# Short-convolution sums in PSUM, long taps in channel pairs, VectorE alone subtracting late in the mixers, router constants split

## The chip, the cores and the metric

The kernel runs on one core of a Trainium2 chip. The metric is the device time of one execution in microseconds, lower is better. Each kernel is timed several times; the median is quoted.

## What is computed

One layer of a streaming encoder on 256 tokens of 1024 channels. Three token mixers read the same input, are merged by sigmoid gates, and pass through one output projection; after a layer norm a routed mixture of 16 experts follows. The part that the change touches:

```python
a = a_val * jax.nn.sigmoid(a_gate)                       # mixer A
a = causal_depthwise_conv(a, conv_a_w) + conv_a_b        # 31 taps
a = jax.nn.silu(layer_norm(a, ln_a_g, ln_a_b))
y_a = jnp.einsum("btc,cd->btd", a, w_a_out)

yb = gate_bb * causal_depthwise_conv(gate_cc * xb, conv_b_w)   # mixer B, 3 taps
y_b = jnp.einsum("btc,cd->btd", yb, w_b_out)

merged = g[..., 0, :] * y_a + g[..., 1, :] * y_b + g[..., 2, :] * y_c
return jnp.einsum("btd,de->bte", merged, w_o) + b_o
```

Mixer C (trailing means, then a grouped projection) gives `y_c`. The router's logits, after the first layer norm, are computed with the norm's gain and shift folded into constants, which `router_consts` makes from the weights alone.

## The kernel before

Channels lie on partitions, in 8 tiles of 128; a row of a tile is the 256 tokens. The mixers run over 49 weight chunks of 1 MB each (list `MIX`), one block of TensorE work per chunk: blocks 0 to 7 are A (each gives value and gate of one channel tile), 8 to 11 are C, then X0 X1 B0 X2 X3 B1 X4 X5 B2 X6 X7 B3 (blocks 12 to 23: an X block gives `gate_cc` and `xb` of one tile, a B block `gate_bb` of two), WC (24), four rounds of two gate blocks and one WB (25 to 36), four more gate blocks G0 (37 to 40), WA0 and WA1 (41, 42), WO0, WA2, WA3, WO1 to WO3 (43 to 48). The experts follow.

Precision is kept by splitting float32 into two halves of a narrower kind: for each chunk, `convert(j + 2, CUT)` at block j has ScalarE copy the high half (line 162), and GpSimd and VectorE subtract it from the raw chunk (line 172) into a low half. Of the 2048 columns of a chunk GpSimd takes the first `CUT` = 1280 (1024 + 256), VectorE the other 768. A block (`proj`) is then 48 matmuls of 128x256: high by high, high by low (line 314) and low by high (line 319), into one PSUM bank of the tag `pj`, of which there are four. A later block can only start when the bank that it reuses has been read.

Who reads the bank of a block:

- A: ScalarE's sigmoid, then VectorE's product (line 346) into `UP`. Of each second A block, 62 conv taps (31 for each of two channel tiles) are queued in `later["V"]`: line 333 for the first tap, 336 for the others. After every block `drain("V", ...)` emits some of the queued taps; how many is a budget of 5.0 us less VectorE's subtraction and less `COST[kind]`. The sum of a channel tile stands in a PSUM bank of its own, tag `z`, `CA[i]`, four banks in turn.
- X (`ev_X`): ScalarE adds a bias (line 393), VectorE multiplies (line 396, this frees the bank), then makes the 3-tap convolution in SBUF: line 400 for the first tap, 402 for the two others.
- B (`ev_B`): VectorE, two instructions at line 407, from the bank times the convolution; then ScalarE and GpSimd split the product.

Mixer A's layer norm (`ln_a`) is placed by `LNA` = 32: the mean's matmul after block 33, centring (lines 458, 459) at block 34, the sum of squares (463) at 35, the variance matmul (468) behind block 35, the scaling (473 to 481) at block 36 and the eight swish steps (`swish`: lines 486 and 487 on VectorE, split by ScalarE at 266 and GpSimd at 267 into `AH` and `AL`) behind blocks 36 and 37. WA0, block 41, is the first to read `AH` and `AL`. `load_res`, `residual` (line 555) and `router_consts` (products and sums on VectorE, 563 to 567, one matmul, 569, and two small operations behind it) hang on `LNA` as well: `router_consts` runs behind block 40.

In the mixers a scheduler orders the instructions of each engine by its own estimate of when they can run; in the experts the order is the program's. Weights are loaded by SyncE's queue, a chunk as soon as the slot of an earlier one is free.

Of the kernel before, what the change touches and what calls it, by code (L numbers as in the profile page):

```python
# [12 lines left out]
AF = mybir.ActivationFunctionType  # L13
OP = mybir.AluOpType
# [3 lines left out]
T = 256  # L18
D = 1024
KT = 8  # L20
NE = 16
# [8 lines left out]
PB, PCW, PCB, PLG, PLB, PBW, PCS, PRT, P1G, P1B = 0, 72, 320, 328, 336, 344, 368, 376, 504, 512  # L30
# [82 lines left out]
def body(ctx, tc, w, xt, x, par, rows, out):  # L113
    nc = tc.nc
    V, S, G, PE = nc.vector, nc.scalar, nc.gpsimd, nc.tensor
# [6 lines left out]
    def slot(tag, shape, dt=F32):  # L122
        nm[0] += 1
        return big.tile(shape, dt, name=f"{tag}_{nm[0]}", tag=tag)

    def t2k(shape, dt=F32, tag="t2k", bufs=5):
        nm[0] += 1
        return tmp.tile(shape, dt, name=f"{tag}_{nm[0]}", tag=tag, bufs=bufs)

    def bank(tag="pj", shape=(128, 2, 256)):  # L130
        nm[0] += 1
        return ps.tile(list(shape), F32, name=f"{tag}_{nm[0]}", tag=tag, bufs=4)
# [19 lines left out]
    def hi(j, a, b, step=512, eng=None):  # L152

        if j not in htag:
            htag[j] = (hfree or free).pop(0)
            HI[j] = slot(htag[j], [128, 2048], F32R)
        for i in range(a, b, step):
            o = slice(i, min(i + step, b))
            if eng:
                eng.tensor_copy(HI[j][:, o], raw[j][:, o])  # L160
            else:
                S.activation(HI[j][:, o], raw[j][:, o], AF.Copy)  # L162

    def lo(j, eng, a, b, step=512):

        if j not in LO:
            ltag[j] = (lfree or free).pop(0)
            LO[j] = slot(ltag[j], [128, 2048], F32R)
        for i in range(a, b, step):
            o = slice(i, min(i + step, b))  # L170
            left[j] = left.get(j, 2048) - (o.stop - o.start)
            eng.tensor_tensor(LO[j][:, o], raw[j][:, o], HI[j][:, o].bitcast(F32), op=OP.subtract)  # L172
        if j in left and left[j] == 0:
            del raw[j], left[j]
            give(tags[j])

    def convert(j, cut, step=1024, half=None):

        if j not in raw:
            return  # L180
        for e in (0, 1) if half is None else (half,):
            a, m, b = 1024 * e, 1024 * e + min(1024, max(0, cut - 1024 * e)), 1024 * e + 1024
            hi(j, a, b, step)
            lo(j, G, a, m, step)
            lo(j, V, m, b, step)
# [33 lines left out]
    def col(base, i):  # L219
        return P[:, base + i:base + i + 1]  # L220
# [44 lines left out]
    def halves(dh, dl, src, eng):  # L265
        S.activation(dh, src, AF.Copy)  # L266
        eng.tensor_tensor(dl, src, dh.bitcast(F32), op=OP.subtract)  # L267
# [17 lines left out]
    def put(eng, cost, f):  # L285
        later[eng].append((cost, f))
# [35 lines left out]

    ssum = [None]

    CA = {}

    def conv_tap(i, k):

        src = UP[:, i, k:k + T]
        wk = P[:, PCW + i * TAPS + k:PCW + i * TAPS + k + 1]  # L330
        if k == 0:
            CA[i] = bank("z", (128, T))
            V.tensor_scalar(CA[i], src, wk, col(PCB, i), op0=OP.mult, op1=OP.add)
        else:
            ca = CA[i]
            V.scalar_tensor_tensor(AC[:, i] if k == TAPS - 1 else ca, src, wk, ca, op0=OP.mult, op1=OP.add)  # L336
        if k == TAPS - 1 and i == 1:
            ssum[0] = t2k([128, T], tag="ssum", bufs=2)
            put("G", 0.6, lambda: G.tensor_tensor(ssum[0], AC[:, 0], AC[:, 1], op=OP.add))
        elif k == TAPS - 1 and i:  # L340
            put("G", 0.6, lambda: G.tensor_tensor(ssum[0], ssum[0], AC[:, i], op=OP.add))
# [41 lines left out]
            put("G", 1.25, lambda lev=lev: add(lev))  # L383
        put("G", 10, mean)

    yconv = {}
    Y = {}

    def ev_X(i, p):
        if i == 0:  # L390
            Y["h"], Y["l"] = slot("YH", [128, KT, T], F32R), slot("YL", [128, KT, T], F32R)
        cc = t2k([128, T])
        S.activation(cc, p[:, 0], AF.Identity, bias=col(PB, 24 + i))
        u = t2k([128, 2 + T])
        G.memset(u[:, :2], 0.0)
        V.scalar_tensor_tensor(u[:, 2:], p[:, 1], col(PB, 32 + i), cc, op0=OP.add, op1=OP.mult)  # L396
        if i % 2 == 0:
            yconv[i // 2] = t2k([128, 2, T])
        y = yconv[i // 2][:, i % 2]
        V.tensor_scalar(y, u[:, :T], col(PBW, 3 * i), None, op0=OP.mult)  # L400
        for k in (1, 2):
            V.scalar_tensor_tensor(y, u[:, k:k + T], col(PBW, 3 * i + k), y, op0=OP.mult, op1=OP.add)

    def ev_B(q, p):
        y = yconv.pop(q)
        for n in range(2):
            V.scalar_tensor_tensor(y[:, n], p[:, n], col(PB, 16 + 2 * q + n), y[:, n], op0=OP.add, op1=OP.mult)
        halves(Y["h"][:, 2 * q:2 * q + 2], Y["l"][:, 2 * q:2 * q + 2], y, G)

    MS = {}  # L410
# [86 lines left out]
    A = {}  # L497
# [26 lines left out]

    done = None
    CUT = 1280
    LNA = 32
    extra, blk = {}, [0]

    def at(j, f, after=False):  # L530

        extra.setdefault((j, after), []).append(f)

    COST = {"A": .45, "C": .7, "X": 1.3, "B": .9, "WB": .7, "WA": 1.3}

    R1 = {}

# [19 lines left out]
    RT = {}  # L557

    def router_consts():

        gw = RT["w"] = const.tile([128, KT, NE], F32, name="gw")
        wr = P[:, PRT:PRT + 128].rearrange("p (k e) -> p k e", e=NE)
        V.tensor_tensor(gw, wr, P[:, P1G:P1G + KT, None].to_broadcast([128, KT, NE]), op=OP.mult)
        bw, bs = t2k([128, KT, NE]), t2k([128, 2, NE])
        V.tensor_tensor(bw, wr, P[:, P1B:P1B + KT, None].to_broadcast([128, KT, NE]), op=OP.mult)
        V.tensor_reduce(bs[:, 0], bw.rearrange("p k e -> p e k"), axis=AX.X, op=OP.add)
        V.tensor_reduce(bs[:, 1], gw.rearrange("p k e -> p e k"), axis=AX.X, op=OP.add)
        pb = bank("pj", (128, 2, NE))
        PE.matmul(pb, ones, bs, start=True, stop=True)
        RT["b"] = const.tile([128, NE], F32, name="rb")  # L570
        V.scalar_tensor_tensor(RT["b"], pb[:, 0], float(D), R1["br"], op0=OP.mult, op1=OP.add)
        RT["s"] = const.tile([128, NE], F32, name="rs")
        V.tensor_scalar(RT["s"], pb[:, 1], float(D), None, op0=OP.mult)

    cost = 0
    for j, c in enumerate(MIX):
        kind, n = c
        blk[0] = j
        if j + 2 < NM:
            convert(j + 2, CUT)  # L580
        if done:
            done()
            done = None
        for f in extra.pop((j, False), ()):
            f()
        cost = 0
        if kind == "WC":
            wc_block(j)
        elif kind == "WO":
            if n == 0:  # L590
                for t in range(2):
                    for half in range(2):
                        wo(j, n, t, half)
        else:
            ah, al = {"WA": lambda: (A["h"], A["l"]), "WB": lambda: (Y["h"], Y["l"])}.get(kind, lambda: (XH, XL))()
            p = proj(j, ah, al)
            f = {"A": ev_A, "C": ev_C, "X": ev_X, "B": ev_B, "WA": ev_WA, "WB": ev_WB}.get(kind)
            done = (lambda f=f, n=n, p=p: f(n, p)) if f else (lambda b=int(kind[1]), n=n, p=p: gate(b, n, p))
            cost = COST.get(kind, 0)
        for f in extra.pop((j, True), ()):  # L600
            f()
        drain("V", 5.0 - (2048 - CUT) * 1.04e-3 - cost)
        drain("G", 5.0 - CUT * 2.2e-3)
        if j == LNA:
            drain("V", 1000)
            drain("G", 1000)
            at(j + 1, lambda: ln_a(LNA + 2), True)
        if j == LNA + 6:
            load_res()
            at(j + 2, router_consts, True)  # L610
            at(j + 2, scaled_identity, True)
            at(j + 3, lambda: residual(0), True)
            at(j + 4, lambda: (residual(1), give("AC")), True)
        if c == ("G0", 3):
            give("XH", "XL")
        if c == ("WA", 3):
            give("AH", "AL")
        if c == ("WO", 1):
            give("PL", "M")
# [437 lines left out]
    j = NM  # L1057
# [47 lines left out]
    for e in range(NE + 1):  # L1105
        if e < NE:
            while e // 2 not in ready:
                some()
            p = bank("pj", (128, 512))
# [64 lines left out]
    y = t2k([128, 512])  # L1174
# [47 lines left out]
    with tc.If(over > CAP):  # L1222
        xs, xt_ = slot(free.pop(0), [128, 2, D]), slot(free.pop(0), [128, KT, T])
        V.tensor_tensor(xs, XX["h"].bitcast(F32), XX["l"].bitcast(F32), op=OP.add)
        z = slot(free.pop(0), [128, 2, D])
# [4 lines left out]
        for t in range(2):  # L1230
            for h in range(2):
                p = bank("pj", (128, 4, 128))
# [3 lines left out]
        for e in range(NE):  # L1236
# [4 lines left out]
            for t in range(2):  # L1241
                gu = []
                for kind in ("EG", "EU"):
                    p = bank("pj", (128, 512))
# [9 lines left out]
                p = bank("pj", (128, 4, 128))  # L1254
# [3 lines left out]
                for b in range(2):  # L1258
                    p = bank("pj", (128, 512))
# [31 lines left out]
```

## Time and profile before

| | |
|---|---|
| median of 3 runs | 633.08 us (632.39 to 633.84) |
| the profiled execution | 633.34 us, its span 631.6 us |
| TensorE busy | 585.9 us, 93% of the span |
| VectorE busy | 569.9 us, 90% |
| ScalarE busy | 373.8 us, 59% |
| GpSimd busy | 254.1 us, 40% |
| granted TensorE clock, mean | 0.97 of full speed |

A busy TensorE counts matmuls as they overlap; what the kernel loses is read from where TensorE idles or runs at the lower clock.

### The profile page before, as it was taken

Reading aid. Unit: us, or ns where it says so; the run is one execution under the profiler, and the core shown is the slowest. Engines: PE = TensorE matmul, PEld = TensorE weight load, DVE = VectorE, ACT = ScalarE, POOL = GpSimd, SP = SyncE. Lnnn points to the kernel's source line nnn. Section 1 sums busy time; section 2 is a strip of 40 time slices with the busy share of each in tenths; the row PEclk is TensorE's granted clock in tenths of the full one; section 3 lists DMA queues with packets and bytes.
Section 4 is the critical chain, followed back from the end, with each engine's and each line's share of the span. In section 5 each row is a group of like instructions: output and inputs, shape, how many; then the busy total and the mean of one; then the engine's idle time right before and its main releaser. Section 6 shows DMA issues by size and latency. Waiting matters only on the chain. (4 is left out here: it accounts for less than half of the span.)

```text
span 631.6 us, 9552 instructions
## 1 busy us (share of the span) xinstructions
PE 585.9 (93%) x3556; PEld 485.5 (77%) x3556; DVE 569.9 (90%) x851; ACT 373.8 (59%) x536; POOL 254.1 (40%) x187
## 2 busy tenths in 40 slices
PE   8999999988799999799989897999999999999990
PEld 6999999978799999798776564766676666666650
DVE  5999999999996399997688989899999999999985
ACT  5644444344344455734336587688778887887861
POOL 3876998874499777966341004000000000000003
PEclk9999999989799999999979899999999999999996
DMA  8985354354357544596753588689979998999101
GB/s 314 421 348 195 141 174 160 134 183 150 134 201 267 191 171 174 188 377 218 315 200 130 204 313 326 246 323 382 423 302 371 381 420 319 388 379 352 67 1 71
DMA packets 24084, 158.77 MB, mean 251 GB/s; under 512 B 2784, under 2 KB 3040, under 8 KB 5472
## 3 DMA queue, kind: packets, MB, share of 16 engines
q1 hardware_dynamic: 24032, 158.10, 65.5%
q8 instruction: 30, 0.49, 0.3%
q14 instruction: 22, 0.18, 0.1%
HBM read 157.04 MB, written 1.05 MB: 250 GB/s over the span
## 5 line engine op out<-in xcount | busy, mean ns | idle before, releaser
L172 POOL TENSOR_TENSOR L<-R,H 128x1024 fp32r<-128x1024 f32 (+1 forms) x72 | 131.9, 1854 | 31.0 <-ACT H L162 30.7
L314 PE MATMUL pj<-XH,H 128*128 128x256 f32 x560 | 139.3, 286 | 3.2 <-DVE t2k L396 3.2
L314 PE MATMUL pj<-XL,H 128*128 128x256 f32 x560 | 139.0, 285 | 0.0
L162 ACT ACTIVATE H<-R 128x1024 fp32r<-128x1024 f32 (+1 forms) x84 | 78.6, 988 | 63.7 <-issue 34.0
L314 PEld LDWEIGHTS pj<-XH,H 128*128 128x128 f32 x560 | 108.8, 194 | 3.4 <-DVE t2k L396 3.4
L314 PEld LDWEIGHTS pj<-XL,H 128*128 128x128 f32 x560 | 108.8, 194 | 0.0
L336 DVE SCALAR_TENSOR_TENSOR z<-UP,par,z 128x256 f32<-128x256 f32 x232 | 97.3, 477 | 0.2
L1192 POOL TENSOR_TENSOR sm<-sm,mhalf 128x1 f32<-128x1 f32 x2 | 1.1, 552 | 227.0 <-DVE sm L1191 227.0
L319 PE MATMUL pj<-XH,L 128*128 128x256 f32 x560 | 78.6, 283 | 0.0
L319 PEld LDWEIGHTS pj<-XH,L 128*128 128x128 f32 x560 | 72.4, 192 | 0.0
L172 DVE TENSOR_TENSOR L<-R,H 128x768 fp32r<-128x768 f32 (+2 forms) x37 | 56.4, 1526 | 9.9 <-ACT H L162 9.9
L172 POOL TENSOR_TENSOR L<-S,H 128x1024 fp32r<-128x1024 f32 (+1 forms) x28 | 49.8, 1800 | 12.5 <-ACT H L162 12.5
L162 ACT ACTIVATE H<-S 128x1024 fp32r<-128x1024 f32 x28 | 28.0, 1049 | 22.2 <-POOL L L172 12.7
L979 ACT ACTIVATE t2k<-pj 64x512 f32<-64x512 f32 x32 | 19.1, 596 | 19.4 <-PE pj L972 17.2
L172 DVE TENSOR_TENSOR L<-S,H 128x768 fp32r<-128x768 f32 x14 | 22.6, 1616 | 3.9 <-ACT H L162 3.9
L267 POOL TENSOR_TENSOR AL<-UP,R 128x512 fp32r<-128x512 f32 x4 | 7.4, 1860 | 45.4 <-ACT R L266 45.4
L981 DVE TENSOR_TENSOR t2k<-pj,t2k 64x512 f32<-64x512 f32 x32 | 21.7, 677 | 1.8 <-ACT t2k L979 1.7
L1000 ACT ACTIVATE hs<-ssum 128x256 fp32r<-128x256 f32 x16 | 6.7, 417 | 22.5 <-DVE ssum L997 22.5
L1014 PEld LDWEIGHTS z<-t2k,pt 128*128 128x128 f32 x64 | 10.9, 188 | 11.4 <-ACT hs L1000 7.3
L1014 PE MATMUL z<-t2k,pt 128*128 128x512 f32 x64 | 18.9, 416 | 0.0
L314 PE MATMUL pj<-AH,H 128*128 128x256 f32 x64 | 17.1, 302 | 0.0
L314 PE MATMUL pj<-AL,H 128*128 128x256 f32 x64 | 17.0, 298 | 0.0
(479 smaller groups left out, 1458.1 us busy)
## 6 DMA issues: line engine op xcount, KB each, us to landing
R<-w SPq DMA_DIRECT2D x55, 1024.0 KB, 5.4
S<-w SPq DMA_DIRECT2D x24, 1024.0 KB, 5.5
H<-w SPq DMA_DIRECT2D x15, 1024.0 KB, 7.6
L<-w SPq DMA_DIRECT2D x7, 1024.0 KB, 6.6
XL<-w SPq DMA_DIRECT2D x6, 1024.0 KB, 7.7
XH<-w SPq DMA_DIRECT2D x6, 1024.0 KB, 8.1
AC<-w SPq DMA_DIRECT2D x6, 1024.0 KB, 7.0
AH<-w SPq DMA_DIRECT2D x6, 1024.0 KB, 7.9
```

What stands on the lines that cost most here:

```text
L162: S.activation(HI[j][:, o], raw[j][:, o], AF.Copy)
L172: eng.tensor_tensor(LO[j][:, o], raw[j][:, o], HI[j][:, o].bitcast(F32), op=OP.subtract)
L267: eng.tensor_tensor(dl, src, dh.bitcast(F32), op=OP.subtract)
L314: PE.matmul(p[:, c], h[:, o:o + 128], m[:, k0 + k], start=(n == 0), stop=False)
L319: PE.matmul(p[:, c], l[:, o:o + 128], ah[:, k0 + k], start=False, stop=(n == 3 * nk))
L336: V.scalar_tensor_tensor(AC[:, i] if k == TAPS - 1 else ca, src, wk, ca, op0=OP.mult, op1=OP.add)
L979: S.activation(t, p[64:], AF.Copy)
L981: V.tensor_tensor(GU[e, n], p[:64], t, op=OP.add)
L1000: S.activation(HS[e][:, :, 0], HF[e], AF.Copy)
L1014: PE.matmul(acc[t, b], PTs[e][:, t], YV[e, b][n], start=False, stop=(e == NE - 1 and n == 1))
L1192: G.tensor_tensor(mv[:, 2:3], mv[:, 1:2], mhalf, op=OP.pow)
```

## The change

1. The sums of mixer A's convolution: two `z` banks, each with a pair of channel tiles, in place of one bank per tile (`ZC`).
2. `ev_X` writes its 3-tap sums into two other `z` banks (`ZY`) instead of SBUF.
3. `ev_B`: ScalarE adds the bias from the bank into SBUF (two activations), VectorE multiplies both tiles by the sums in one 128x512 instruction.
4. `COST["X"]` goes from 1.3 to 2.2, so that fewer taps are emitted behind an X block.
5. `LNA` goes from 32 to 34: the layer norm of A, the residual's load and sums, and the last drain of the queued taps come two blocks later. WA0 stays block 41.
6. From block `LNA` on, `convert` gives GpSimd no columns: chunks 36 to 48 are subtracted by VectorE alone, two instructions of 128x1024 instead of one of 128x768.
7. `router_consts` keeps the products and sums (now behind block 42); the matmul and what follows go to `router_consts2`, behind block 45.

```diff
-    CA = {}
+    ZC = [bank("z", (128, 2, T)) for _ in range(2)]
+    ZY = [bank("z", (128, 2, T)) for _ in range(2)]
...
         if k == 0:
-            CA[i] = bank("z", (128, T))
-            V.tensor_scalar(CA[i], src, wk, col(PCB, i), op0=OP.mult, op1=OP.add)
+            V.tensor_scalar(ZC[i // 2 % 2][:, i % 2], src, wk, col(PCB, i), op0=OP.mult, op1=OP.add)
         else:
-            ca = CA[i]
+            ca = ZC[i // 2 % 2][:, i % 2]
...
-        if i % 2 == 0:
-            yconv[i // 2] = t2k([128, 2, T])
-        y = yconv[i // 2][:, i % 2]
+        y = ZY[i // 2 % 2][:, i % 2]
...
     def ev_B(q, p):
-        y = yconv.pop(q)
+        y = t2k([128, 2, T])
         for n in range(2):
-            V.scalar_tensor_tensor(y[:, n], p[:, n], col(PB, 16 + 2 * q + n), y[:, n], op0=OP.add, op1=OP.mult)
+            S.activation(y[:, n], p[:, n], AF.Identity, bias=col(PB, 16 + 2 * q + n))
+        V.tensor_tensor(y, y, ZY[q % 2], op=OP.mult)
...
-    LNA = 32
+    LNA = 34
...
-    COST = {"A": .45, "C": .7, "X": 1.3, "B": .9, "WB": .7, "WA": 1.3}
+    COST = {"A": .45, "C": .7, "X": 2.2, "B": 0.9, "WB": .7, "WA": 1.3}
...
-        pb = bank("pj", (128, 2, NE))
+        RT["bs"] = bs
+
+    def router_consts2():
+        pb, bs = bank("pj", (128, 2, NE)), RT["bs"]
         PE.matmul(pb, ones, bs, start=True, stop=True)
...
-            convert(j + 2, CUT)
+            convert(j + 2, CUT if j < LNA else 0)
...
             at(j + 2, router_consts, True)
+            at(j + 5, router_consts2, True)
```

VectorE around the evacuation of X0 (396 before, 395 now). `z` are the conv sums, `pj` a block's bank, `t2k` a buffer in SBUF, `UP` the input of the long convolution. Before:

```order
L396 SCALAR_TENSOR_TENSOR t2k_1093<-pj_1021,par,t2k_1091 128x256
L336 SCALAR_TENSOR_TENSOR z_785<-UP_132,par,z_785 128x256
L336 SCALAR_TENSOR_TENSOR z_1385<-UP_132,par,z_1385 128x256
L336 SCALAR_TENSOR_TENSOR z_1383<-UP_132,par,z_1383 128x256
L336 SCALAR_TENSOR_TENSOR z_848<-UP_132,par,z_848 128x256
L400 TENSOR_SCALAR t2k_1096<-t2k_1093,par 128x256
```

And now:

```order
L395 SCALAR_TENSOR_TENSOR t2k_1091<-pj_1021,par,t2k_1089 128x256
L336 SCALAR_TENSOR_TENSOR z_172<-UP_132,par,z_172 128x256
L333 TENSOR_SCALAR z_171<-UP_132,par 128x256
L397 TENSOR_SCALAR z_173<-t2k_1091,par 128x256
L336 SCALAR_TENSOR_TENSOR z_172<-UP_132,par,z_172 128x256
L336 SCALAR_TENSOR_TENSOR z_171<-UP_132,par,z_171 128x256
L399 SCALAR_TENSOR_TENSOR z_173<-t2k_1091,par,z_173 128x256
```

The taps go round four buffers before and alternate between two (each a pair of tiles) now. Ahead of X0's evacuation stood 119 taps and now stand 109; between those of X0 and X7 stood 78 and now stand 75, beside 10 subtractions in both.

VectorE at the layer norm of A, from the centring to the scaling. `AC` is the convolution's result, `PH` its squares, `L` and `R` and `H` a chunk's low half, raw words and high half. Before:

```order
L172 TENSOR_TENSOR L_229_2611<-R_193_2145,H_228_2609 128x768
L458 TENSOR_TENSOR AC_170<-AC_170,t2k_2622 128x1024 x2
L463 TENSOR_REDUCE t2k_2689<-PH_2608 128x256
L172 TENSOR_TENSOR L_235_2679<-R_198_2215,H_234_2677 128x768
L473 TENSOR_SCALAR t2k_2755<-pj_2740 128x256
L172 TENSOR_TENSOR L_242_2744<-R_203_2288,H_241_2742 128x768
L475 RECIPROCAL t2k_2756<-t2k_2754 128x256
```

And now (lines two lower):

```order
L172 TENSOR_TENSOR L_235_2732<-R_199_2272,H_234_2730 128x1024 x2
L456 TENSOR_TENSOR AC_170<-AC_170,t2k_2741 128x1024 x2
L442 TENSOR_TENSOR t2k_2804<-pj_2747,t2k_2675 128x512
L172 TENSOR_TENSOR L_241_2798<-R_204_2344,H_240_2796 128x1024 x2
L461 TENSOR_REDUCE t2k_2808<-PH_2729 128x256
L172 TENSOR_TENSOR L_248_2863<-S_209_2414,H_247_2861 128x1024
L471 TENSOR_SCALAR t2k_2873<-pj_2859 128x256
L172 TENSOR_TENSOR L_248_2863<-S_209_2414,H_247_2861 128x1024
L473 RECIPROCAL t2k_2874<-t2k_2872 128x256
```

Between the centring and the sum of squares there now stand an evacuation of a WB block and a whole chunk's subtraction.

TensorE around WA0. Before, the router's matmul stands between block 40 (`pj_3073`) and WA0 (`pj_3151`):

```order
L319 MATMUL pj_3073<-XH_136,L_273_2935 128x256 x8
L569 MATMUL pj_3129<-t2k_3125,ones 128x32
L314 MATMUL pj_3151<-AH_2763,H_280_3002 128x256
L314 MATMUL pj_3151<-AL_2764,H_280_3002 128x256
L314 MATMUL pj_3151<-AH_2763,H_280_3002 128x256
```

Now WA0 is `pj_3129` and WA1 `pj_3193`:

```order
L314 MATMUL pj_3129<-AH_2881,H_265_2961 128x256
L314 MATMUL pj_3129<-AL_2882,H_265_2961 128x256
L314 MATMUL pj_3129<-AH_2881,H_265_2961 128x256
L314 MATMUL pj_3193<-AH_2881,H_277_3048 128x256
L314 MATMUL pj_3193<-AL_2882,H_277_3048 128x256
L314 MATMUL pj_3193<-AH_2881,H_277_3048 128x256
L314 MATMUL pj_3129<-AL_2882,H_265_2961 128x256
L314 MATMUL pj_3193<-AL_2882,H_277_3048 128x256
L314 MATMUL pj_3129<-AH_2881,H_265_2961 128x256
```

From its fourth matmul on WA0 alternates with WA1, 15 matmuls of which stand ahead of WA0's last of the first 16. The router's matmul has gone behind WA3; the variance matmul, which stood behind block 35, stands behind block 37.

## Rows read from the trace of the kernel before

**Rows 1.** Windows of 10 us: busy (x instructions) by engine, PEclk, DMA share, GB/s.

```profile
130.00:140.00 10.00, 6.85 (x45) 6.75 (x44) 10.00 (x20) 3.11 (x5) 6.73 (x5) 0.83 0.40 129
140.00:150.00 10.00, 10.00 (x86) 10.00 (x85) 10.00 (x19) 4.26 (x5) 4.89 (x5) 1.00 0.40 147
150.00:160.00 10.00, 5.41 (x44) 5.00 (x42) 10.00 (x19) 4.35 (x8) 6.74 (x5) 1.00 0.50 170
160.00:170.00 10.00, 8.51 (x49) 8.51 (x50) 10.00 (x20) 3.57 (x6) 3.85 (x3) 0.66 0.54 200
...
200.00:210.00 10.00, 10.00 (x86) 10.00 (x85) 4.22 (x3) 4.74 (x6) 8.64 (x6) 1.00 0.48 163
```

**Rows 2.** TensorE's timeline, blocks 1 to 24: start, us, instruction, idle before and releaser.

```profile
19.54 1.12 PE L319 MATMUL pj<-XH,L 128*128 128x256 f32 x8
...
128.98 1.12 PE L319 MATMUL pj<-XH,L 128*128 128x256 f32 x8
133.25 0.48 PE L314 MATMUL pj<-XH,H 128*128 128x256 f32 x1 [3.15 <-DVE t2k L396]
...
153.24 0.50 PE L422 MATMUL pj<-PH,H 128*128 128x256 f32 x2 [0.96 <-DVE t2k L396]
...
161.49 0.80 PE L422 MATMUL pj<-PH,H 128*128 128x256 f32 x2 [5.12 <-DVE t2k L396]
```

**Rows 3.** VectorE's timeline: evacuations of X0, X4 and X7.

```profile
90.72 0.47 DVE L396 SCALAR_TENSOR_TENSOR t2k<-pj,par,t2k 128x256 f32<-128x256 f32 x1
...
132.72 0.47 DVE L396 SCALAR_TENSOR_TENSOR t2k<-pj,par,t2k 128x256 f32<-128x256 f32 x1
...
160.97 0.47 DVE L396 SCALAR_TENSOR_TENSOR t2k<-pj,par,t2k 128x256 f32<-128x256 f32 x1
```

**Rows 4.** VectorE's instructions by line and form: busy us, mean ns, idle before.

```profile
L336 DVE SCALAR_TENSOR_TENSOR z<-UP,par,z 128x256 f32<-128x256 f32 x232 | 97.3, 477 | 0.2
L172 DVE TENSOR_TENSOR L<-R,H 128x768 fp32r<-128x768 f32 x33 | 51.3, 1554 | 9.1 <-ACT H L162 9.1
...
L402 DVE SCALAR_TENSOR_TENSOR t2k<-t2k,par,t2k 128x256 f32<-128x256 f32 x16 | 15.8, 985 | 0.0
...
L506 DVE TENSOR_TENSOR M<-M,t2k 128x512 f32<-128x512 f32 x4 | 9.8, 2440 | 0.1
...
L486 DVE TENSOR_SCALAR t2k<-AC,par 128x256 f32<-128x256 f32 x8 | 7.2, 924 | 0.3
...
L333 DVE TENSOR_SCALAR z<-UP,par 128x256 f32<-128x256 f32 x8 | 4.3, 539 | 0.1
...
L172 DVE TENSOR_TENSOR R<-AC,H 128x1024 fp32r<-128x1024 f32 x2 | 2.4, 1222 | 0.0
```

**Rows 5.** Line 400 alone: shortest, median and longest in ns.

```profile
L400 DVE TENSOR_SCALAR t2k<-t2k,par x8: 343/864/1744, 92.7 to 163.3; 128x256 f32<-128x256 f32 x8
```

**Rows 6.** VectorE's timeline: three taps on one sum; three that alternate between two.

```profile
18.35 1.54 DVE L336 SCALAR_TENSOR_TENSOR z<-UP,par,z 128x256 f32<-128x256 f32 x3
...
22.67 1.26 DVE L336 SCALAR_TENSOR_TENSOR z<-UP,par,z 128x256 f32<-128x256 f32 x3
```

**Rows 7.** TensorE's timeline late in the mixers.

```profile
231.94 0.67 PE L468 MATMUL pj<-t2k,ones 128*128 128x256 f32 x2 [0.99 <-DVE t2k L463]
...
260.26 1.12 PE L319 MATMUL pj<-XH,L 128*128 128x256 f32 x8
265.79 0.38 PE L569 MATMUL pj<-t2k,ones 128*128 128x32 f32 x2 [4.40 <-DVE t2k L567]
...
272.96 1.12 PE L319 MATMUL pj<-AH,L 128*128 128x256 f32 x8
...
300.24 0.74 PE L519 MATMUL z<-H,YH 128*128 128x512 f32 x2 [1.16 <-ACT YH L266]
```

**Rows 8.** VectorE's timeline: the scaling of mixer A's layer norm.

```profile
238.89 4.37 DVE L481 TENSOR_TENSOR AC<-AC,t2k 128x2048 f32<-128x2048 f32 x1
```

**Rows 9.** GpSimd's timeline: the last low half of WA's input.

```profile
265.44 0.73 POOL L267 TENSOR_TENSOR AL<-t2k,AH 128x256 fp32r<-128x256 f32 x1
```

More of the change, by code (lines that the diff above doesn't have):

```diff
@@ L384, in ev_C @@
         put("G", 10, mean)
-    yconv = {}
     Y = {}
```

## The prediction

> **What bounds the kernel now.** I first cut the span into windows and looked for those in which TensorE runs fewer matmuls than it can. A full window of 10 us holds 86 [rows 1]. Three windows, 130 to 140, 150 to 160 and 160 to 170 us, hold 45, 44 and 49, which is 120 too few; at 10 / 86 = 0.116 us each that is 13.9 us. In two of them the granted clock is 0.83 and 0.66, a mix of 2.4 and 1.2 GHz: part of the loss is work at the lower level behind the waits. VectorE is busy for 10.00 of 10 us in all four, GpSimd and ScalarE are not: this stretch belongs to VectorE. In 200 to 210 us VectorE is busy for 4.22 only: later it has room.
>
> Then TensorE's timeline, for the waits. The last eight matmuls of block 1 begin at 19.54 and those of block 20 at 128.98 us [rows 2]: 109.44 us for 19 blocks, 5.76 each (48 matmuls 0.12 apart), so nothing is lost until then. Block 1 ends 8 x 0.12 later, at 20.50, and block k would at that pace end at 14.74 + 5.76 k. After block 20 come waits of 3.15, 0.96 and 5.12 us, together 9.23, all ended by an evacuation of an X block at line 396 [rows 2]. With the lower clock the stretch costs about 14, a factor of 1.5 on its waits.
>
> VectorE's timeline says how late it is there: X0 (block 12, end 83.86) is evacuated from 90.72, X4 (block 18, end 118.42) from 132.72, X7 (block 22, unhindered end 141.46) from 160.97 [rows 3]. The lag grows from 6.9 to 14.3 to 19.5 us: between X0 and X7 VectorE has 70.25 us of work where TensorE has ten blocks, 57.6 us. WC follows B3, and its second group is halfway into the groups' work, so X7 may lag by about 5.76 + 2.88 = 8.6 us before WC waits.
>
> Last the end of the mixers: 0.99 us before the variance matmul, 4.40 before the router's matmul, 1.16 in WO [rows 7]. WA0's last eight matmuls begin at 272.96 and those of block 40 at 260.26, 12.70 us apart where 5.76 (and 0.4 for the router's matmul) would do: 6.5 us are lost around WA0.
>
> **The X blocks (parts 1 to 4).** Between X0 and X7 stood 7 first products at line 400 and 13 sums at line 402, and stand 7 and 14. Line 400 takes from 343 to 1744 ns with a median of 864 [rows 5], line 402 takes 985 on average [rows 4]; the same arithmetic with its sum in PSUM, lines 333 and 336, takes 539 and 477 and hardly varies [rows 4, 6]. So I take out 7 x 0.86 + 13 x 0.985 = 18.8 us and put in 7 x 0.54 + 14 x 0.48 = 10.5: 8.3 less. The bounds: the old prices (nothing won) and, if 402 falls to the 0.39 at which alternating taps follow each other [rows 6], 9.5. Three taps fewer: 1.3. B's evacuation was two instructions per block, about the 0.47 of line 396, and is one of twice the columns: between 0 and 1 won over three blocks, I take 0.7. Sum 10.3 us, so 60 us between X0 and X7 against TensorE's 57.6.
>
> Ahead of X0 stand 10 taps fewer, 4.2 us with the 0.42 between the two spacings of rows 6. If VectorE stays as full as it was, X0 lags by 6.9 - 4.2 = 2.7; if it idles early instead, by 6.9. X7 then lags by 5 to 9 us, against 8.6 allowed, and the blocks between may lag by three whole blocks. The waits of 9.23 us go, all but 0.4 at the worst, and with them the lower clock: **-14 us** (bounds -13.5 and -14 with these prices; the old prices are rival A). ScalarE's two extra passes per B block, taken as the 0.47 of line 396 each, lie beside 3 to 5 busy us in 10 [rows 1]; without that room they would delay the bank by about 1 us.
>
> The trace shows, in rows 4 and 5, that line 400 at its shortest (343 ns) beats line 333 at its usual (539): undisturbed, the SBUF form is quicker. The Trainium skill, page "VectorE: DVE Perf Modes", section "Why PSUM operands drop a tier", says the same as a rule: an operand in PSUM keeps a float32 operation at the single rate. By it alone, with 343 for each line 400, the seven would lose 1.4 us instead of winning 2.3, X7's lag would be 9 to 13, and the sum up to 6 us higher, 3 in the middle. I go by the median: beside a busy GpSimd the short form is the exception.
>
> **The layer norm two blocks later (5), the router's matmul (7).** Two costs and two gains.
>
> Variance matmul: between the centring and the sum of squares there now stand an evacuation of a WB block (about 0.7) and two subtractions of 1.22 [rows 4], and ScalarE's squares take 1.2 of that time anyway; the centring gains about as much as its own chunk's subtraction costs more. I take 2.3 us of wait instead of 0.99: **+1.3** (bounds 0 and +3.1).
>
> WA0: before, from the variance matmul (231.94) to the last low half of WA's input (265.44 + 0.73) it took 34.2 us [rows 7, 9], under five blocks (28.8). Now only three blocks (17.3 us) lie above it. But the chain shrinks, since GpSimd no longer runs subtractions beside it. The scaling took 4.37 us for 2048 columns [rows 8], where VectorE with GpSimd idle takes 1.22 for 1024 [rows 4]: -1.9. The eight steps at line 486 took 924 ns against the 343 of an undisturbed instruction of that shape [rows 4, 5]: -4.6. The low halves queue no more behind two subtractions on GpSimd: -3. VectorE's own subtraction rises from 1.55 to 2.44 for four chunks: +3.6. That is about 28, less what lines 487 and the waits between engines shorten: 25 to 28. Behind the 17.3 us TensorE can do 30 matmuls, 15 of WA0 and 15 of WA1, before the last half is due: 3.6. What is left to wait is 4 to 7 us, with the lower clock 5 to 8, against 6.5 lost before: **0** (bounds -2 and +2). The 4.40 us in front of the router's matmul are in the 6.5: when it goes, the swish is what is late.
>
> **VectorE alone (6).** 13 chunks at 2.44 instead of 1.55 us are 11.6 us more on VectorE, but spread over 75 us in which it has room (window 200 to 210), and line 506, 2.44 us a piece beside GpSimd [rows 4], should come near 0.6 for its 512 columns. It stands in front of WO's wait of 1.16: **-0.7** (bounds -1.2 and 0). If the cover were gone the 11.6 us would show in full. The expert phase keeps its order and only starts earlier.
>
> **Sum.** 633.3 (profiled execution; the median of the runs is 0.3 lower) - 14 + 1.3 + 0 - 0.7 = 619.9. I forecast 620.
>
> **Rivals.** *A, the 3-tap sums stay dear.* If lines 397 and 399 cost what 400 and 402 cost, because their input is still in SBUF, X7 lags by 19.5 - 4.2 - 2 = 13.3; WC waits 4.7 us, with the clock 7, and half of the gain is gone: 627. Against it: line 336 also reads SBUF and averages 477. *B, the chain to WA0 does not shrink.* 34.2 us under 17.3 + 3.6 leaves 13.3, with the clock some 15 where 6.5 were lost: 628. For it: VectorE's blocks 36 to 41 are nearly full with the larger subtractions. *C, taps on a shared pair wait for each other (slower than before).* Three taps in a row on one sum take 0.51 us each, three that alternate 0.39 [rows 6]. If two taps that alternate between the two pairs, or between two tiles of one pair, count as dependent, each of the 184 taps up to X7 costs 0.12 more, 22 us: X7 lags by 5 + 22 = 27, WC waits 18, with the clock 27, 13 more than the 14 of before: 646. It decides from about 0.07 us per tap, where X7's lag reaches 17.9 and the old 9.23 us of waits are back. Against it: the pairs alternate in the new order at the distance that already gave 0.39. *D, nothing waits.* If the chain to WA0 falls to 21 us as well, 6 more go: 614. *E, the change doesn't thin the stretch:* 75 taps for 78 show that the higher cost of X hardly moves taps, so part 4 is worth 1.3 us and the rest hangs on the price of the sums, which is rival A.
>
> **How the numbers follow.** Forecast 0.62 (its bounds 617 to 624), A 0.10 (the page's rule half-way to it), B 0.12, C 0.07, D 0.09. From 614 to 628 C, half of D and the worse half of B are left out, somewhat under 2 in 10. Within 0.2% of before, about what a measurement of this kernel can tell from no change, falls only a mixture of A and B (0.03); with both and the bounds against it, or C, it is slower: 0.08; faster 0.89.
>
> **What would show it.** Right: no matmul wait over 1 us between 20 and 167 us and a granted clock of 1.00 there; lines 397 and 399 at 0.54 and 0.48; X7's evacuation 5 to 9 us behind its block; lines 479 near 2.5 and 484 near 0.4 us; one wait of 4 to 7 us spread over WA0's first matmuls. Wrong: taps of 0.51 (C), sums near 1 us (A), a wait above 10 us ended by `AH` or `AL` (B), or any wait for a low half made by VectorE after block 36, which would mean that its room there was not enough.

## The result, and the profile after

The changed kernel takes 617.51 us (median of 4 runs, 616.45 to 618.56) against 633.46 for the kernel before in the runs beside it: a ratio of 0.9745, interval 0.9716 to 0.9775. The forecast was 620. The profiled execution took 618.56 us with a span of 616.8.

The windows that answer to [rows 1], of the changed kernel (busy by engine, PEclk, DMA share, GB/s):

```profile
130.00:140.00 10.00, 10.00 (x86) 10.00 (x85) 10.00 (x24) 2.74 (x4) 7.01 (x6) 1.00 0.58 206
...
150.00:160.00 10.00, 10.00 (x86) 10.00 (x85) 10.00 (x24) 6.50 (x13) 5.56 (x4) 1.00 0.62 218
...
250.00:260.00 10.00, 8.06 (x43) 6.77 (x42) 7.02 (x11) 6.66 (x14) 5.42 (x6) 0.76 0.99 374
```

The windows that held 45, 44 and 49 matmuls are full, at the full clock. VectorE is as full as it was; it no longer falls further behind. What is left is the window of WA0, 250 to 260 us. VectorE's evacuations of X0 and X7, as in [rows 3]:

```profile
93.53 0.47 DVE L395 SCALAR_TENSOR_TENSOR t2k<-pj,par,t2k 128x256 f32<-128x256 f32 x1
...
151.34 0.48 DVE L395 SCALAR_TENSOR_TENSOR t2k<-pj,par,t2k 128x256 f32<-128x256 f32 x1
```

Between them lie 57.8 us where there were 70.25. Block 0 ends at 17.20 us in this execution (at 14.74 before), so X0 is 7.2 us behind its block and X7 7.4: the lag is there, but it does not grow any more. The groups that answer to [rows 4, 5]:

```profile
L399 DVE SCALAR_TENSOR_TENSOR z<-t2k,par,z 128x256 f32<-128x256 f32 x16 | 7.7, 479 | 0.0
L484 DVE TENSOR_SCALAR t2k<-AC,par 128x256 f32<-128x256 f32 x8 | 4.5, 596 | 0.1
...
L397 DVE TENSOR_SCALAR z<-t2k,par 128x256 f32<-128x256 f32 x8 | 3.8, 476 | 0.0
...
L504 DVE TENSOR_TENSOR M<-M,t2k 128x512 f32<-128x512 f32 x4 | 2.7, 685 | 0.0
```

The 3-tap sums went from 985 to 479 ns and their first products from 864 (median) to 476; WA's sum into `M` from 2440 to 685, with GpSimd quiet. The late waits of TensorE, as in [rows 7], and the last low half of WA's input, as in [rows 9]:

```profile
232.95 0.70 PE L466 MATMUL pj<-t2k,ones 128*128 128x256 f32 x2 [2.16 <-DVE t2k L461]
...
253.03 0.50 PE L314 MATMUL pj<-AH,H 128*128 128x256 f32 x2 [0.67 <-ACT AH L266]
254.75 0.50 PE L314 MATMUL pj<-AL,H 128*128 128x256 f32 x2 [1.22 <-POOL AL L267]
...
288.88 0.74 PE L517 MATMUL z<-H,YH 128*128 128x512 f32 x2 [0.34 <-ACT YH L266]
289.96 0.73 PE L517 MATMUL z<-H,YL 128*128 128x512 f32 x2 [0.34 <-DVE YL L267]
```

```profile
257.33 1.41 POOL L267 TENSOR_TENSOR AL<-t2k,AH 128x256 fp32r<-128x256 f32 x2 [1.01 <-ACT AH L266]
```

The milestones of TensorE cut the span into stretches. For before and after:

| stretch | before | after | difference | forecast |
|---|---|---|---|---|
| start to the end of block 0 | 14.74 | 17.20 | +2.5 | 0 |
| from there to the end of WC | 152.04 | 138.24 | -13.8 | -14 |
| blocks 25 to 40 | 94.44 | 95.32 | +0.9 | +1.3 |
| WA0 and WA1 | 17.86 | 17.56 | -0.3 | 0 |
| from there to the first transpose behind WO | 40.05 | 39.18 | -0.9 | -0.7 |
| experts, to the end of the span | 312.47 | 309.30 | -3.2 | 0 |

The four rows of the mixers moved by 14.1 us where the sum said 13.4; the first and the last row were in no term of it. In the second profiles of both kernels (below) the same four rows come to 292.4 us for the change and 306.6 for before, 14.1 apart again, though blocks 25 to 40 alone take 96.8 and 94.1 there.

### The profile page after: what moved, and what is told of

Read it like the earlier page. It is cut to its first block, busy times and chain, and to the rows that moved or that the text cites. A ratio compares the mean times of both kernels' runs of the same rounds, so it can differ in the third digit from the quotient of the medians.

```text
span 616.8 us, 9526 instructions
## 1 busy us (share of the span) xinstructions
PE 580.4 (94%) x3556; PEld 480.0 (78%) x3556; DVE 550.9 (89%) x860; ACT 377.4 (61%) x544; POOL 207.0 (34%) x161
## 5 line engine op out<-in xcount | busy, mean ns | idle before, releaser
L314 PE MATMUL pj<-XH,H 128*128 128x256 f32 x560 | 137.5, 283 | 0.0
L314 PE MATMUL pj<-XL,H 128*128 128x256 f32 x560 | 137.4, 283 | 0.0
L314 PEld LDWEIGHTS pj<-XL,H 128*128 128x128 f32 x560 | 107.5, 192 | 0.0
L314 PEld LDWEIGHTS pj<-XH,H 128*128 128x128 f32 x560 | 107.5, 192 | 0.0
L172 POOL TENSOR_TENSOR L<-R,H 128x1024 fp32r<-128x1024 f32 (+2 forms) x54 | 93.5, 1754 | 23.2 <-ACT H L162 23.2
L336 DVE SCALAR_TENSOR_TENSOR z<-UP,par,z 128x256 f32<-128x256 f32 x232 | 98.8, 479 | 0.7
L172 DVE TENSOR_TENSOR L<-R,H 128x768 fp32r<-128x768 f32 (+2 forms) x46 | 64.9, 1424 | 11.8 <-ACT H L162 11.8
L172 POOL TENSOR_TENSOR L<-S,H 128x1024 fp32r<-128x1024 f32 (+1 forms) x20 | 36.6, 1851 | 1.2 <-ACT H L162 1.2
L172 DVE TENSOR_TENSOR L<-S,H 128x768 fp32r<-128x768 f32 (+1 forms) x18 | 26.6, 1483 | 3.2 <-ACT H L162 3.1
L1016 PE MATMUL z<-t2k,pt 128*128 128x512 f32 x64 | 18.8, 415 | 0.0
```

The source lines that it names most:

```text
L314: PE.matmul(p[:, c], h[:, o:o + 128], m[:, k0 + k], start=(n == 0), stop=False)
L1016: PE.matmul(acc[t, b], PTs[e][:, t], YV[e, b][n], start=False, stop=(e == NE - 1 and n == 1))
```

## The experiments

Eleven runs in three groups, each compared with the kernel before on the same chip.

**The change once more, the two halves of it, and LNA back.** First the change alone.

> The changed kernel once more, for its time beside the experiments. The profile of before has its experts (first transpose behind WO to the end) in 312.5 us, that of the change in 309.3; block 0 ends at 14.74 and at 17.20 us. Theory 1 (both are the granted clock of one execution): this profile shows other values, block 0 ending nearer 14.7 and the experts anywhere from 309 to 313; the time is 616 to 619. Theory 2 (both are effects of the change): block 0 ends near 17.2 again and the experts take 309.3 again.

It takes 618.2 us, 0.9754 (0.9724 to 0.9784). Block 0 ends at 13.91 us, so the late start of the first profile was that execution's, as theory 1 said; the experts take 309.8 us, nearer to theory 2, and are taken up below.

Parts 1 to 4 alone: the diff above up to `COST`, with `LNA` at 32 and `convert` and `router_consts` as before.

> The kernel before with parts 1 to 4 alone (sums in PSUM, pairs, B's product, cost of X). Theory 1 (the gain is VectorE's lag in the X blocks): 14 us less than before, 0.978, no wait of TensorE between 20 and 155 us, and the 4.4 us before the router's matmul still there. Theory 2 (parts 5 to 7 win 3 us, in the experts or in the tail, and the X blocks only 11): 0.982 or more.

618.6 us, 0.9757 (0.9725 to 0.9789): the whole of the change. From block 0 to the end of WC it takes 138.24 us, 24 blocks of 5.76 to the hundredth. The wait before the router's matmul is in place:

```profile
251.96 0.60 PE L567 MATMUL pj<-t2k,ones 128*128 128x32 f32 x2 [4.41 <-DVE t2k L565]
```

Parts 5 to 7 alone:

> The kernel before with parts 5 to 7 alone (layer norm two blocks later, VectorE alone from there, router split). Theory 1: within 2 us of before, 0.998 to 1.003, with the waits of 9.2 us in the X blocks and WC as before, the variance matmul waiting about 2.2 us and WA0 losing about 6. Theory 2 (they win in the experts): 3 us less than before, 0.995, the experts in 309 us.

632.4 us, 0.998 (0.9954 to 1.0005): no difference that can be told. The waits in the X blocks and WC are 3.16, 2.49 and 5.13 us (the middle one was 0.96 in the first profile of before and is 2.50 in its second), the variance matmul waits 2.16, WA0 0.66 and 1.22, as in the change. Theory 1 holds; the experts' 310.3 us are taken up below.

The change with the layer norm back where it was:

```diff
-    LNA = 34
+    LNA = 32
...
-            convert(j + 2, CUT if j < LNA else 0)
+            convert(j + 2, CUT if j < 34 else 0)
...
-            at(j + 2, router_consts, True)
-            at(j + 5, router_consts2, True)
+            at(j + 4, router_consts, True)
+            at(j + 7, router_consts2, True)
```

> The changed kernel with LNA back at 32, VectorE alone still from chunk 36 on and the router's parts at the blocks where the change has them. Theory 1 (the two blocks later cost what the lighter chain wins): from the variance matmul to the last low half takes about 25 us as in the changed kernel, now under five blocks, so the 6 us lost around WA0 go: 611 to 613, 0.966 of before. Theory 2 (VectorE has no room for the chain and the larger subtractions at once): the chain stretches to 30 us or more or a low half comes late; less than 2 us won on the changed kernel, or a loss.

612.0 us, 0.9657 (0.9626 to 0.9689). TensorE has no wait left at WA0. Of its timeline and GpSimd's:

```profile
218.84 0.67 PE L466 MATMUL pj<-t2k,ones 128*128 128x256 f32 x2 [1.66 <-DVE t2k L461]
```

```profile
246.40 2.37 POOL L267 TENSOR_TENSOR AL<-t2k,AH 128x256 fp32r<-128x256 f32 x2 [1.88 <-ACT AH L266]
```

The last low half is ready at 248.77, 29.9 us behind the variance matmul, not 25: the chain does stretch, but under five blocks that costs nothing. Theory 1 gave the time, theory 2 the length of the chain.

**One part undone at a time.** The 3-tap sums in SBUF again, and with them B's product in two instructions of VectorE (parts 2 and 3):

```diff
...
-        y = ZY[i // 2 % 2][:, i % 2]
+        if i % 2 == 0:
+            yconv[i // 2] = t2k([128, 2, T])
+        y = yconv[i // 2][:, i % 2]
...
-            S.activation(y[:, n], p[:, n], AF.Identity, bias=col(PB, 16 + 2 * q + n))
-        V.tensor_tensor(y, y, ZY[q % 2], op=OP.mult)
+            V.scalar_tensor_tensor(y[:, n], p[:, n], col(PB, 16 + 2 * q + n), y[:, n], op0=OP.add, op1=OP.mult)
```

> The changed kernel with the 3-tap sums back in SBUF and B's product in VectorE's two instructions (parts 2 and 3 undone; pairs, cost and parts 5 to 7 stay). Theory 1 (the price of these sums is the gain): VectorE has some 9 us more between X0 and X7, X7's lag goes from 7.4 to about 16 us, WC waits about 8 and with the lower clock loses 12: 628 to 631, 0.993 of before. Theory 2 (pairs and the cost of X give the gain): under 3 us slower than the change, 0.980 or less.

632.0 us, 0.9978 (0.9954 to 1.0002), a little above the range of theory 1: without these two parts nothing that can be told is left of the change. Its waits in WC and VectorE's two groups:

```profile
155.10 0.69 PE L421 MATMUL pj<-PH,H 128*128 128x256 f32 x2 [3.02 <-DVE t2k L395]
162.71 0.58 PE L421 MATMUL pj<-PH,H 128*128 128x256 f32 x1 [4.79 <-DVE t2k L395]
```

```profile
L401 DVE SCALAR_TENSOR_TENSOR t2k<-t2k,par,t2k 128x256 f32<-128x256 f32 x16 | 16.2, 1010 | 0.0
L399 DVE TENSOR_SCALAR t2k<-t2k,par 128x256 f32<-128x256 f32 x8 | 10.2, 1275 | 0.0
```

The waits are 7.8 us where 8 were expected, and the stretch up to WC is 12.75 us longer than 138.24 where 12 were expected. X7 is 18 us behind its block, not 16.

Why the sums are dear in SBUF can be read instruction by instruction. Of the 16 at line 401, the eight that run while GpSimd does nothing take 472 to 475 ns; the eight that run beside an instruction of GpSimd take 783 to 2543. One of each kind, and GpSimd beside the first (two subtractions, the first of which ends at 159.54):

```profile
157.20 3.20 POOL L172 TENSOR_TENSOR L<-S,H 128x1024 fp32r<-128x1024 f32 x2
```

```profile
157.35 2.47 DVE L401 SCALAR_TENSOR_TENSOR t2k<-t2k,par,t2k 128x256 f32<-128x256 f32 x1
...
160.53 0.47 DVE L401 SCALAR_TENSOR_TENSOR t2k<-t2k,par,t2k 128x256 f32<-128x256 f32 x1
```

In the changed kernel the sums in PSUM (line 399) take 475 to 488 ns, whether GpSimd works beside them or not.

The cost of X at 1.3 again:

> The changed kernel with the cost of X back at 1.3 (part 4 undone). In the order of VectorE 104 taps stand ahead of X0 and 73 between X0 and X7, where the change has 109 and 75. Theory 1: X7's lag stays under 8.6 us and nothing waits: as the change, within 1.5 us, 0.973 to 0.978. Theory 2 (the change rests on fewer taps behind X blocks): WC waits 1 us or more, 2 us slower than the change.

619.45 us, 0.9771 (0.9727 to 0.9815). X0 is 7.2 us behind its block and X7 7.5, as in the change, and 138.24 us lead to WC's end. The expectation's 104 and 73 taps are not what ran: the profile has 109 taps ahead of X0 and 75 up to X7, and on every engine the same operations on the same names in the same order as in the change. So, as far as the profile tells buffers apart, part 4 left the order as it was, and it has no share.

GpSimd's 1280 columns to the end (`convert(j + 2, CUT)`):

> The changed kernel with GpSimd taking its 1280 columns to the end (part 6 undone). Theory 1 (the chain to WA0 is short because GpSimd is quiet): from the variance matmul to the last low half of WA's input it is 33 to 35 us again instead of 25.8, under three blocks, so WA0 loses 8 us more: 626, 0.988 of before. Theory 2 (the chain is set by VectorE's own work, of which there is then less): chain 24 to 28 us, the time within 2 us of the change.

626.0 us, 0.988 (0.9838 to 0.9922), the time of theory 1, but only part of it where that theory put it. TensorE's waits at WA0 and in WO, and the last low half on GpSimd:

```profile
258.19 0.58 PE L314 MATMUL pj<-AL,H 128*128 128x256 f32 x1 [2.36 <-POOL AL L267]
288.44 0.51 PE L517 MATMUL z<-L,YH 128*128 128x512 f32 x1 [1.08 <-POOL L L172]
293.13 1.22 PE L517 MATMUL z<-H,YH 128*128 128x512 f32 x2 [2.69 <-ACT YH L266]
```

```profile
257.22 2.47 POOL L267 TENSOR_TENSOR AL<-t2k,AH 128x256 fp32r<-128x256 f32 x3
```

The chain is 30.1 us (229.61 to 259.69), not 33 to 35. From the end of block 40 to the first transpose behind WO it takes 66.84 us instead of 56.74: 3.8 of these 10.1 lie up to WO's first matmul, 6.3 in the rest, with waits of 1.08 us for a low half made by GpSimd and 2.69 for a high half of ScalarE, which had waited for VectorE's sum into `M` (2.55 us there beside GpSimd, 0.69 in the change). In return the variance matmul waits 0.66 us where it waits 2.16 in the change.

The kernel before once more, for its profile (span 634.4 us):

> The kernel before once more, for its profile: in its first profile and in that of parts 1 to 4 alone the granted clock falls in the router (the 16 gather matmuls take 3.8 us) and again some 30 us later, and the experts take 312 us; in the four profiles with parts 5 to 7 neither falls there together and they take 309 to 310. Theory 1 (chance of the execution): this profile shows another pattern, with the experts under 311. Theory 2 (parts 5 to 7 set it): both falls again, 312 us.

The pattern is another, but the experts take 312.1 us. Neither theory is met; see below.

**Three more.** The layer norm one block earlier still, with the variance matmul, the scaling and the swish one block further from the sum of squares:

```diff
-        at(j + 1, var, True)
-        at(j + 2, rstd)
+        at(j + 2, var, True)
+        at(j + 3, rstd)
...
-    LNA = 34
+    LNA = 31
...
```

> As the kernel with LNA at 32 (612.0), with LNA at 31 and the variance matmul, the scaling and the swish one block further from the sum of squares, so that the swish stands where it stood and the variance matmul has a block more of cover. Theory 1 (the wait of 1.7 us and the lower clock behind it, 2.7 us between WC and WA0, go): 609 to 610.5, no wait of TensorE over 0.4 us between 20 and 275 us. Theory 2 (VectorE is then late elsewhere): a wait at a low half or at AL takes its place, 612 or more.

612.8 us, 0.9677 (0.9647 to 0.9706), no faster than with `LNA` at 32. The waits are gone as theory 1 said (no wait over 0.4 us between 20 and 275 us), blocks 25 to 40 take 92.91 us instead of 94.81, and the first transpose comes 1.9 us sooner, counted from block 0. The lower clock that the expectation put behind the wait was not there: with `LNA` at 32 the granted clock is 1.00 from 20 to 280 us, and the wait was all that could be won. Its profile gives that back in the experts: 312.1 us against 309.3.

Rival C made real:

```diff
-    ZC = [bank("z", (128, 2, T)) for _ in range(2)]
+    ZC = [bank("z", (128, 2, T))] * 2
```

> The changed kernel with one bank instead of two for the pairs, so that no two pairs alternate: rival C made real. Its order has 84 taps ahead of X0, 64 between X0 and X7 and 100 behind. Rival C as it was priced (0.12 us more per tap, all of it in front of WC): 640 or more. Theory 1 (0.52 us per tap, but the scheduler has moved taps behind X7): X7 lags by about 11 us, WC waits 2 to 3, the taps end some 25 us later where VectorE has room: 619 to 624.

628.7 us, 0.9934 (0.9904 to 0.9963), between the two theories and met by neither. X7 is evacuated at 148.23 us, 6.7 behind its block, and WC does not wait at all. TensorE stops later, at the mean of the layer norm; its wait, GpSimd's work that ended it, and eight taps on VectorE:

```profile
225.82 1.22 PE L448 MATMUL pj<-ssum,ones 128*128 128x256 f32 x2 [9.34 <-POOL ssum L341]
```

```profile
224.24 1.52 POOL L341 TENSOR_TENSOR ssum<-ssum,AC 128x256 f32<-128x256 f32 x2 [4.18 <-DVE AC L336]
```

```profile
181.26 4.15 DVE L336 SCALAR_TENSOR_TENSOR z<-UP,par,z 128x256 f32<-128x256 f32 x8
```

Eight taps of one pair take 4.15 us, 0.52 each behind the first. The scheduler has put 100 taps behind X7 where the change has 64; they end at 224.6 us, too late for the layer norm.

The router's constants in one piece again:

> The changed kernel with the router's constants in one piece again, behind block 42 (part 7 undone; the matmul stands between WA1 and WA2). Theory 1 (the wait of 4.4 us was only cover for the late swish): within 1.5 us of the change, 617 to 619.5, the matmul waiting for less than 1 us. Theory 2 (the matmul stops TensorE for VectorE's products and sums wherever it stands): a wait of 2 to 4 us, 621 or more.

619.2 us, 0.9793 (0.9751 to 0.9835). The matmul (266.19 us, directly behind WA1's last) waits for nothing. Part 7 has no share that can be told either.

## Why the prediction was right, point by point

- **What bounds.** That VectorE's lag in the X blocks costs 14 us, with a factor of 1.5 on the waits: shown, by parts 1 to 4 alone (the stretch loses nothing) and by the sums in SBUF (waits of 7.8 us cost 12.75, a factor of 1.6).
- **The price of the 3-tap sums.** Line 399 was put at 0.48 us and measures 0.479; line 397 at 0.54 and measures 0.476. VectorE's stretch from X0 to X7 shrank by 12.4 us where 10.3 were forecast. Two terms were mis-sized, by their price from start to start in VectorE's timeline. What was put in, 21 instructions in PSUM, follows at 0.39 us each and comes to 8.2 us, not 10.5. What was taken out, 20 in SBUF, comes to 19.7, not 18.8: for line 400 the working took the median, 864 ns, where a sum over instructions wants the mean (8.8 us over 8 is 1.1). The rest of the work there, fewer taps and B's product among it, won 1.0 us and not 2.0.
- **Ten taps fewer ahead of X0.** Two ends were given, a lag of 2.7 us if VectorE stays full and 6.9 if it idles early. X0 is 7.2 us late, but the idling is only part of the reason. From the first tap to X0 the taps take 3.3 us less than before; in the first profile VectorE idles 2.7 us there (0.1 before), in the second 0.9, and the same 14 subtractions take 20.8 and 20.6 us where they took 18.1. That subtractions would lengthen was not thought of. The result hung on neither end, since X7 stays under 8.6 both ways.
- **The rule against the change.** The shortest first product in SBUF took 343 ns, with the sum in PSUM (line 397) it never came under 471. The Trainium skill's rule (page "VectorE: DVE Perf Modes", section "Why PSUM operands drop a tier") agrees with that and still does not decide: in the SBUF experiment line 399 averages 1275 beside a busy GpSimd. The Trainium skill's page "SBUF — State Buffer", section "SBUF: two separate sides", says that a VectorE instruction with two SBUF inputs and a GpSimd instruction that reads SBUF exclude each other at a shared pair of ports. The 472 to 475 ns of line 401 alone and 783 to 2543 beside GpSimd fit that.
- **Variance matmul, WA0, tail.** 2.3 us of wait forecast, 2.16 measured; a chain of 25 to 28 us, 25.8 measured (to 258.74 us); 0 at WA0, -0.3; -0.7 in the tail, -0.9. The shape at WA0 was another than forecast. WA0 and WA1 take 17.56 us, 6.0 more than with `LNA` at 32, where nothing waits, and 5 to 8 were forecast; but the waits shown are 1.9 us and not 4 to 7, and the granted clock is 0.50 from 255.2 to 262.0 us. The pieces of the chain were 2.29 us for line 479 (near 2.5 forecast) and 0.60 for line 484 (near 0.4). That VectorE's 11.6 us are hidden: no matmul waits for a chunk's low half that it made. The 0.34 us in WO are for the low half of WA's product, which it made before as well (0.60 us of wait there).
- **The rivals.** A fell on the price. Its mechanism is real, as the SBUF experiment shows, and its time was too low (627, measured 632 with B's product undone as well): it counted 4.2 us of lag as won ahead of X0, which is 7.2 us late there too. B fell: the chain shrank. C's premise holds within a pair and not between pairs, and its place was wrong: with one pair the scheduler moves the taps and the wait turns up at the layer norm. D, put at 614 for a chain under its cover, is what `LNA` at 32 does: 612, with a chain that is longer and has more cover. E gave part 4 the three taps; with X at 1.3 again they stay away all the same.
- **What was not in the sum.** The experts, which "only start earlier", took 3.2 us less. In the 13 profiles their length falls into two groups: 311.7 to 312.9 us (before twice, parts 1 to 4, sums in SBUF, GpSimd late, one pair, `LNA` 31) and 309.3 to 310.3 (the change twice, parts 5 to 7, cost of X, router whole, `LNA` 32). Behind the wait of 2.8 us early in the experts all 13 agree, at 239.0 to 239.7. The difference lies ahead of it and goes with the granted clock. The 16 gather matmuls take 3.76 us in the first profile of before and 2.02 in that of the change, with the same instructions in the same order, but they don't separate the groups: with the sums in SBUF (312.9 us) they take 2.02 as well. What separates them is the stretch that ends with the wait of 2.8 us and begins, some 38 us behind the first transpose, with the end of one of 2.2 us. It takes 34.1 to 35.5 us in the seven longer profiles and 32.5 in the six shorter ones. Near its start the clock falls to the lower level in all of the seven and in none of the six. For before and for the change, from about 36 us behind the first transpose:

```profile
355.00:365.00 10.00, 7.78 (x24) 4.82 (x25) 7.80 (x12) 4.69 (x8) 0.00 (x0) 0.83 0.41 135
```

```profile
343.00:353.00 10.00, 8.19 (x29) 4.88 (x30) 8.77 (x14) 7.32 (x11) 0.00 (x0) 1.00 0.62 213
```

With parts 5 to 7 in, both lengths occur (309.3 with `LNA` 32; 312.1 with 31, 312.9 with the sums in SBUF, 311.7 with one pair), so they do not set it by themselves; without them only the longer one was seen, in three profiles. Why the clock falls there in some profiles and not in others, and whether those parts have a share in it, stays open, and with it how much of the 2.5 us between 620 and 617.5 is theirs.

## What to carry to other kernels

When an engine is full and late, read how its lag grows from one evacuation to the next: the saving needed is what stops the growth, and what the bound can give back is the waits and the lower clock behind them. Price an instruction that shares a resource by its mean beside the other engine, from start to start, not by its shortest or its median; the undisturbed minimum speaks for the wrong form. A change made of seven edits may rest on a few: without the two that moved the short sums nothing is left of it (they were not parted from each other, nor from the pairs, which free the banks), and one of the others, the later layer norm, hid 6 us that `LNA` at 32 with the other late parts gives.

## What was not expected of the hardware

Taps that alternate between the two halves of one pair's buffer follow each other at the spacing of taps on one sum. In the changed kernel, eight taps that go round both pairs and eight of the last pair alone:

```profile
172.49 3.22 DVE L336 SCALAR_TENSOR_TENSOR z<-UP,par,z 128x256 f32<-128x256 f32 x8
...
183.07 4.15 DVE L336 SCALAR_TENSOR_TENSOR z<-UP,par,z 128x256 f32<-128x256 f32 x8
```

That is 0.39 and 0.52 us each behind the first, as in [rows 6] for two sums and one. Whether the chip or a wait that the program sets for the whole buffer makes the difference was not tried.

The start is not steady: in the first profile of the change the clock is at its lower level from 9.43 to 16.26 us, while block 0 runs, and block 0 ends at 17.20 us; in the second the clock does not fall there, and it ends at 13.91. The wait of 1.23 us ahead of the fall does not explain it alone: with one pair TensorE waits 1.15 us there and the clock stays up.
